# The ring of the near branch's value tiles: eight buffers in place of six

## The chip, the cores and the metric

The kernel runs on one core of one Trainium2 chip. The metric is device time in microseconds (us): the median of three runs before the change is 2152.53 (2151.78 to 2155.79).

## The reference: what is computed

A trunk of two residual layers over 1024 tokens of width 1024, all in fp32. Layer 0 mixes tokens with a chunked gMLP (mixer A) and with dilated sliding-window attention (mixer B), layer 1 with gated linear attention; behind each mixer stands a gated MLP with a short causal convolution. The change lies in mixer B of layer 0, cut here to what matters:

```python
B_HEADS = 8
B_HEAD_DIM = 64
B_BRANCHES = ((128, 1), (512, 4), (2048, 16))
B_BLOCK = 128
...
    qh = rms_norm(heads(q), q_g)
    kh = rms_norm(heads(k), k_g)
    vh = heads(vb).astype(jnp.float32)
    outs, lses = [], []
    for window, dilation in B_BRANCHES:
        o_r, l_r = dilated_branch(qh, kh, vh, window, dilation)
        outs.append(o_r)
        lses.append(l_r)
    wts = jax.nn.softmax(jnp.stack(lses), axis=0)
    o = jnp.einsum('rbhs,rbhsc->bhsc', wts, jnp.stack(outs))
    b_out = o.transpose(0, 2, 1, 3).reshape(Bn, S, B_WIDTH)
    return jnp.concatenate([a_out, b_out], axis=-1).astype(h.dtype) @ w_out
```

Each query sees a band of keys (its own block of 128 and the one before, at a stride), once for each branch; the branches' outputs are weighted by their denominators. The kernel computes the branch of dilation 1 as the "near" branch, and the two others as one "dilated" branch with a mask that counts them both.

## The kernel before, in words

**Layer 0's mixers** are the function `even` and what it calls. The eight heads go by pairs p = 0 to 3, the 1024 tokens by eight tiles n of 128.

`project(p)` makes q, k and v of a pair: for each token tile, `projected(n)` runs 24 matmuls of 128x384 into a PSUM tile `pj` (L193 at work for `mm_tok`), squares q and k into `qn` on ACT (L780), writes v times the token's norm into the value tile `vN` on ACT (L781 and L782), sends `vN` to a DRAM copy `vd` (L785), and scales q and k on DVE out of `pj` (L787 to L791). The value tiles are a ring: one pool tag `vN` with six buffers for all pairs. `qn` is a ring of five, `pj` one of two.

In the same loop the near branch's unit for tile n follows: splits and transposes of q and k (tiles `tq`, `tk`, L809 and L817), two score matmuls `sc` for each of two heads (L727), the mask and minimum on DVE (L732), the exponential on ACT (L733), transposes `pP` (L747), a copy `pT` (L750 or L752), and the value matmuls `po` (L755), which read `vN` of tiles n-1 and n. So a value tile n is free when the unit of tile n+1 has run.

`dilated(p)` runs eight such units on strided keys, with values `v4` read back from `vd`, into the tiles `ot..d`, and writes them to a DRAM tensor `od` (L849). They are read back in token order as `on` (L887). `combine` and `combined` weigh near and dilated outputs (L858 to L877: small operations on DVE, an exponential on ACT, three large multiplications and additions on DVE and POOL) and write the DRAM tensor `bcat` (L878).

**What fills TensorE beside the attention**: the projections of the next pair (`pj`), and for the last pair the gMLP's two projections `pv` and `pu` (eight tiles of 24 matmuls of 128x512 each, L193), with the small spatial matmuls `pm` (L678). Behind `pu` the output projection begins: `turn` transposes (tile `pc0`, L706) the first token tile's gMLP half (`mx`) and attention half (`cat`, read back from `bcat`, L697), the split into two fp32r parts goes to `hq` (L101 on ACT, L102 on DVE), and the matmuls `po0` follow (L193). `load_half` makes that projection's weights `wo0` by the same split (L101, L102) from DMA loads (L111).

**What sets the order.** The kernel is written with a tile framework that schedules: it lists the instructions of each engine in an order that follows a simulated timeline and the program's order as priority, and puts in the waits. Each engine then runs its own list strictly in order. A tile of a ring can be listed only behind the last reader of the buffer that it takes, so the number of buffers enters the order of every engine. Queue SP issues the DMAs, in order as well.

In the names below a number behind p stands for the pair, the next for the token tile: `pj10` is pair 1, tile 0; `po3d1` is the second output tile of pair 3's dilated branch.

Of the kernel before, what the change touches and what calls it, by code (L numbers as in the profile page):

```python
# [9 lines left out]
F32 = mybir.dt.float32  # L10
# [9 lines left out]
P = 128  # L20
# [23 lines left out]
def f32(ap):  # L44
    return ap.bitcast(F32)
# [6 lines left out]
def rows(t, n):  # L52
    return t[n * P : (n + 1) * P, :]
# [3 lines left out]
def trunk(ctx: ExitStack, tc: tile.TileContext, a, out):  # L57
# [41 lines left out]
    def split(dst, src, hi=None, lo=None):  # L99

        (hi or A.copy)(dst[0], src)  # L101
        (lo or V.tensor_sub)(dst[1], src, f32(dst[0]))  # L102
# [35 lines left out]
    def inv_rms(ssq, cols, n, name, r=None):  # L138
        if r is None:
            r = small.tile([P, cols], F32, tag="rs%d" % cols, name=name)  # L140
        G.tensor_scalar(r, ssq, 1.0 / n, EPS, op0=ALU.mult, op1=ALU.add)  # L141
        G.tensor_tensor(r, r, mhalf[:, :cols], op=ALU.pow)
        return r
# [36 lines left out]
    def tok(n, k):  # L180
        return [hq[k % 2][n // 4][:, i, k // 2, (n % 4) * P : (n % 4 + 1) * P] for i in range(2)]

    def mm_tok(ps, lhs, rhs, nk, amid=None):

        for k in range(nk):
            if amid and k == AMID:
                amid()
            L, R = lhs(k), rhs(k)
            for i in range(2):
                for o, sl in ps:  # L190
                    for ii, jj in PASSES:
                        if ii == i:
                            T.matmul(o, L[i], R[jj][:, sl], start=(k == 0 and (ii, jj) == PASSES[0]),  # L193
                                     stop=(k == nk - 1 and (ii, jj) == PASSES[-1]))
# [423 lines left out]
    def load_qkv(p, wx, between=None):  # L618

        ws = []  # L620
        for kp in range(4):
            raw = load_raw(a["w_qkv"][p, kp], f"wq{p}{kp}r", 768)
            if between:
                between(kp)
            for i in range(2):
                k = 2 * kp + i
                src, gain = raw[:, i * 384 : i * 384 + 384], g0[:, k : k + 1]
                if p % 2 or k >= 4:
                    ws.append(parts_of(src, f"wq{p}{kp}_{i}", gain=gain))
                else:  # L630
                    w = wx.tile([P, 2, 384], F32R, tag="wx", name=f"wx{p}{k}")
                    ws.append([w[:, j, :] for j in range(2)])
                    scaled(ws[-1], src, gain)
        return ws
# [80 lines left out]
    def attention(ps, at, av, pq, pq0, par0, wx, wq0, gqk, masks, rest, gm_open):  # L715
# [3 lines left out]
        def by4(t):  # L719

            return t.rearrange("p s (m r) -> p s r m", r=4)
# [36 lines left out]
        def outputs(name):  # L758
            return (at.tile([P, 4, 132], F32, tag="ot", name="ot" + name, bufs=6),
                    ps.tile([P, 4, P], F32, tag="po", name="po" + name))  # L760

        def project(p, ws=None, then=None, early=None):


            ws = ws or load_qkv(p, wx)
            pool = pq if p % 2 else pq0
            qR = pool.tile([P, 2, S], F32R, tag="qR", bufs=1, name=f"qR{p}")
            kT = pool.tile([P, 4, S], F32R, tag="kT", bufs=1, name=f"kT{p}")
            vd = dram.tile([S, P], F32, name=f"vd{p}")
            vN, os, qns = [], [], []  # L770
            heads = lambda t: t.rearrange("p (h c) -> p h c", c=64)

            def projected(n):

                pj = ps.tile([P, 512], F32, tag="pt" if early and n in (1, 3) else "pj", name=f"pj{p}{n}")
                mm_tok([(pj[:, :384], slice(0, 384))], lambda k: tok(n, k),
                       lambda k: ws[k], KD)
                qn = pq.tile([P, 256], F32, tag="qn", bufs=5, name=f"qn{p}{n}")
                rn = r0[:, n : n + 1]
                A.activation(qn, pj[:, :256], AF.Square, scale=rn)  # L780
                vN.append(pq.tile([P, P], F32, tag="vN", bufs=6, name=f"vN{p}{n}"))  # L781
                got = A.mul(vN[n], pj[:, 256:384], rn)  # L782
                if early:
                    early(n, got)
                Q.dma_start(rows(vd, n), vN[n])  # L785
                ssq = small.tile([P, 4], F32, tag="ss4", name=f"ss{p}{n}")
                V.reduce_sum(ssq, heads(qn), axis=AX.X)  # L787
                r = inv_rms(ssq, 4, 64, f"rq{p}{n}")
                V.scalar_tensor_tensor(heads(qn), heads(pj[:, :256]), rn, r[:, :, None].to_broadcast([P, 4, 64]),
                                       op0=ALU.mult, op1=ALU.mult)  # L790
                G.tensor_tensor(heads(qn[:, :P]), heads(qn[:, :P]), gqk[:, None, :].to_broadcast([P, 2, 64]), op=ALU.mult)  # L791
                qns.append(qn)

            lead = 3 if early else 0
            for n in range(lead):
                projected(n)
            for n in range(NT):
                if n + lead < NT:
                    projected(n + lead)
                qn = qns[n]  # L800
                qs = pq.tile([P, 2, P], F32R, tag="qs", bufs=2, name=f"qs{p}{n}")
                ks = pq.tile([P, 4, P], F32R, tag="ks", bufs=2, name=f"ks{p}{n}")
                split([qs[:, :, :64], qs[:, :, 64:]], heads(qn[:, :P]), hi=G.tensor_copy)
                kk = ks.rearrange("p (h i) (x c) -> p h i x c", i=2, x=2)
                split([kk[:, :, i] for i in range(2)], heads(qn[:, P:])[:, :, None, :].to_broadcast([P, 2, 2, 64]),
                      hi=G.tensor_copy)
                tq = ps.tile([P, 2, P], F32R, tag="tq", name=f"tq{p}{n}")
                for j in range(2):
                    T.transpose(tq[:, j, :], qs[:, j, :], identr)  # L809
                ts_ = slice(n * P, n * P + P)  # L810
                qT = pq.tile([P, 2, P], F32R, tag="qT", bufs=3, name=f"qT{p}{n}")
                A.copy(qT, f32(tq))
                four = lambda t: t.rearrange("p s (r m) -> p s r m", r=4)[:, :, :, 32 * n : 32 * n + 32]
                G.tensor_copy(four(qR), by4(f32(qT)))
                tk = ps.tile([P, 4, P], F32R, tag="tq", name=f"tk{p}{n}")
                for j in range(4):
                    T.transpose(tk[:, j, :], ks[:, j, :], identr)  # L817
                (V.tensor_copy if n % 2 else A.copy)(four(kT), by4(f32(tk)))

                if n % 4 == 0:  # L820
                    ot, po = outputs(f"{p}n{n}")
                    os.append(ot)
                m0 = max(n - 1, 0)
                unit(p, f"{p}n{n}", n % 4, ot, po, lambda s, qT=qT: qT[:, s],
                     lambda s, i: kT[:, 2 * s + i, :].rearrange("p (r m) -> p r m", r=4)[:, :, 32 * m0 : 32 * n + 32],
                     vN[m0 : n + 1], mband, lambda t: t.rearrange("p (m r) -> p r m", r=4))
                if n % 4 == 3:
                    A.copy(ot[:, :, :P], po)
                if then and n in (4, 5):
                    then(n - 4)  # L830
            v4 = av.tile([P, 4, 2, P], F32, tag="v4", name=f"v4{p}", bufs=1)
            for b in range(2):
                Q.dma_start(v4[:, :, b, :], vd.rearrange("(b m r) c -> b m r c", b=2, r=4)[b])
            return os, qR, kT, v4
# [46 lines left out]
        for p in range(PAIRS):  # L881
# [11 lines left out]
            def then(g):  # L893
                weights(g)()
# [470 lines left out]
```

## Time and profile before

| | |
|---|---|
| median of three runs | 2152.53 us |
| the profiled execution | 2153.15 us, its span 2151.4 us |
| PE busy | 2126.6 us (99%), 10444 matmuls |
| DVE, ACT, POOL busy | 1526.0 (71%), 1035.9 (48%), 482.4 us (22%) |
| mixers of layer 0 | from 0 to about 370 us of the span |

The profile is one execution. "Span" runs from the first to the last instruction; what lies around it (1.75 us here) belongs to the run's time. Busy shares are of the span. A matmul's row has a modelled end, so back-to-back matmuls overlap in the list. In the answers by stretches, (x158) is the number of instructions, PEclk the granted share of TensorE's clock, and PEld the loading of weights, which runs beside PE. In the timeline and the chain, a row is start, duration, engine, line and tiles; "SPq" is the issue of a DMA.

### The profile page before, as it was taken

Reading aid. Unit: us, or ns where it says so; the run is one execution under the profiler, and the core shown is the slowest. Engines: PE = TensorE matmul, PEld = TensorE weight load, DVE = VectorE, ACT = ScalarE, POOL = GpSimd, SP = SyncE. Lnnn points to the kernel's source line nnn. Section 1 sums busy time; section 2 is a strip of 40 time slices with the busy share of each in tenths; the row PEclk is TensorE's granted clock in tenths of the full one; section 3 lists DMA queues with packets and bytes.
Section 4 is the critical chain, followed back from the end, with each engine's and each line's share of the span. In section 5 each row is a group of like instructions: output and inputs, shape, how many; then the busy total and the mean of one; then the engine's idle time right before and its main releaser. Section 6 shows DMA issues by size and latency. Waiting matters only on the chain.

```text
span 2151.4 us, 29696 instructions
## 1 busy us (share of the span) xinstructions
PE 2126.6 (99%) x10444; PEld 1804.0 (84%) x10444; DVE 1526.0 (71%) x2451; ACT 1035.9 (48%) x1998; POOL 482.4 (22%) x521
## 2 busy tenths in 40 slices
PE   8999999999999999999999999999999999999999
PEld 7999988888888888888898888888788888888887
DVE  7566655587888888655577777677778888885554
ACT  7555664365444444444454455535544444444443
POOL 5344310012424334000010011011234334220000
PEclk9999999999999999999999999999999999999999
DMA  7022313754444544765553233395554544457664
GB/s 273 24 77 68 104 40 120 256 195 156 155 161 158 176 143 157 255 237 192 206 183 113 74 105 102 133 307 206 177 167 161 168 153 154 162 181 280 215 216 166
DMA packets 159413, 353.70 MB, mean 164 GB/s; under 512 B 17392, under 2 KB 54256, under 8 KB 158880
## 3 DMA queue, kind: packets, MB, share of 16 engines
q1 hardware_dynamic: 159264, 351.81, 47.9%
q8 instruction: 82, 1.34, 0.3%
q14 instruction: 67, 0.55, 0.1%
HBM read 243.15 MB, written 108.59 MB: 163 GB/s over the span
## 4 chain that ended last, share of the span: by engine, by line
PE 92%; DVE 2%; ACT 2%; DMA 2%; issue 1%; SPq 0%; POOL 0%; DVEq 0%; ACTq 0%
PE puB L293 11%; PE pgB L293 11%; PE po L193 8%; PE pv L193 6%; PE pj L193 6%; PE puC L293 6%; PE pgC L293 6%; PE pdB L400 5%; PE pdC L400 5%; PE pdO L400 4%; PE puA L293 3%; PE pgA L293 3%; PE pdQ L400 2%; PE pdP L400 2%; PE pu L193 2%; PE pBq L1070 2%
## 5 line engine op out<-in xcount | busy, mean ns | idle before, releaser
L102 DVE TENSOR_TENSOR da<-ar,da 128x512 fp32r<-128x512 f32 x154 | 106.1, 689 | 154.2 <-ACT da L101 154.1
L101 ACT CAST da<-ar 128x512 fp32r<-128x512 f32 x154 | 95.9, 623 | 207.8 <-PE pdC L400 91.5
L193 PE MATMUL po<-wo,hq 128*128 128x512 f32 x768 | 184.0, 394 | 0.2 <-ACT hq L101 0.2
L193 PEld LDWEIGHTS po<-wo,hq 128*128 128x128 f32 x768 | 141.6, 188 | 29.6 <-DVE hq L102 1.1
L193 PE MATMUL pv<-wv,hq 128*128 128x512 f32 (+2 forms) x768 | 140.8, 340 | 1.6 <-DVE b L1102 1.6
L400 PE MATMUL pdB<-dw,da 128*128 128x512 f32 x528 | 135.5, 391 | 0.9 <-ACT u L308 0.7
L400 PE MATMUL pdC<-dw,da 128*128 128x512 f32 x528 | 135.1, 390 | 0.0
L193 PEld LDWEIGHTS pv<-wv,hq 128*128 128x128 f32 x768 | 118.7, 189 | 16.4 <-DVE b L1102 2.1
L400 PEld LDWEIGHTS pdB<-dw,da 128*128 128x128 f32 x528 | 98.7, 188 | 22.3 <-ACT u L308 1.1
L259 POOL TENSOR_TENSOR S1g<-rg 128x512 f32<-128x512 f32 x20 | 31.1, 1555 | 382.9 <-DMA wsd<-D 266.1
L400 PEld LDWEIGHTS pdC<-dw,da 128*128 128x128 f32 x528 | 99.0, 188 | 20.5
L102 DVE TENSOR_TENSOR dw<-wr,dw 128x512 fp32r<-128x512 f32 x154 | 105.6, 686 | 12.1 <-ACT dw L101 11.9
L193 PE MATMUL pj<-wq,hq 128*128 128x384 f32 x576 | 111.3, 341 | 0.0
L141 POOL TENSOR_SCALAR rn<-ssq 128x1 f32<-128x1 f32 x24 | 9.7, 403 | 446.1 <-ACT h L149 244.9
L101 ACT CAST dw<-wr 128x512 fp32r<-128x512 f32 x154 | 95.0, 617 | 15.7 <-DMA wr<-in_w_dn 9.3
L400 PE MATMUL pdO<-dw,da 128*128 128x512 f32 x396 | 102.2, 389 | 0.2 <-DVE dw L102 0.2
L193 PEld LDWEIGHTS pj<-wq,hq 128*128 128x128 f32 x576 | 99.9, 189 | 0.1
L400 PEld LDWEIGHTS pdO<-dw,da 128*128 128x128 f32 x396 | 74.2, 188 | 16.0 <-DVE dw L102 0.6
L322 DVE SCALAR_TENSOR_TENSOR t<-g,cw,t 128x1022 f32<-128x1022 f32 x44 | 76.6, 1742 | 0.1
L306 DVE TENSOR_TENSOR g<-g,s1g 128x512 f32<-128x512 f32 x22 | 16.2, 737 | 76.9 <-ACT s1g L305 76.9
L321 DVE SCALAR_TENSOR_TENSOR t<-g,cw,t 128x1023 f32<-128x1023 f32 x44 | 58.2, 1322 | 16.2 <-ACT t L320 16.1
L323 ACT ACTIVATE t<-t 128x1024 f32<-128x1024 f32 x44 | 46.7, 1061 | 29.7 <-DVE t L322 29.6
(1084 smaller groups left out, 5432.6 us busy)
## 6 DMA issues: line engine op xcount, KB each, us to landing
ar<-actd SPq DMA_DIRECT2D x70, 512.0 KB, 3.5
rd<-in_w_down SPq DMA_DIRECT2D x44, 512.0 KB, 3.6
wsd<-D SPq DMA_DIRECT2D x88, 256.0 KB, 2.3
rg<-in_w_gate SPq DMA_DIRECT2D x42, 512.0 KB, 3.6
ru<-in_w_up SPq DMA_DIRECT2D x42, 512.0 KB, 4.5
wr<-wsd SPq DMA_DIRECT2D x40, 512.0 KB, 4.3
actd<-t SPq DMA_DIRECT2D x66, 256.0 KB, 2.2
wr<-in_w_dn SPq DMA_DIRECT2D x30, 512.0 KB, 4.8
```

The source lines that it names most:

```text
L101: (hi or A.copy)(dst[0], src)
L102: (lo or V.tensor_sub)(dst[1], src, f32(dst[0]))
L141: G.tensor_scalar(r, ssq, 1.0 / n, EPS, op0=ALU.mult, op1=ALU.add)
L193: T.matmul(o, L[i], R[jj][:, sl], start=(k == 0 and (ii, jj) == PASSES[0]), stop=(k == nk - 1 and (ii, jj) == PASSES[-1]))
L259: G.tensor_tensor(sums[name], x, y, op=op)
L293: T.matmul(o, L[ii][:, j * P : j * P + P], right[p][:, jj, j, :], skip_group_check=more, start=(not more and j == 0 and (ii, jj) == PASSES ...
L306: V.tensor_add(C22, C22, s1)
L321: V.scalar_tensor_tensor(t[:, 1:], g[:, : S - 1], w(1), t[:, 1:], op0=ALU.mult, op1=ALU.add)
L322: V.scalar_tensor_tensor(t[:, 2:], g[:, : S - 2], w(0), t[:, 2:], op0=ALU.mult, op1=ALU.add)
L323: A.activation(t, t, AF.Silu)
L400: T.matmul(o, L[ii][:, t * P : t * P + P], R[jj], skip_group_check=more, start=start and not more and (ii, jj) == PASSES[0], stop=stop and ...
L1070: T.matmul(o, L[ii][:, j * P : j * P + P], right[p][:, jj, j, :], skip_group_check=more, start=(not more and j == 0 and (ii, jj) == PASSES ...
```

## The change

One number: the ring `vN` gets eight buffers of 128x128 fp32 (512 bytes in each partition) in place of six.

```diff
@@ -778,7 +778,7 @@
                 qn = pq.tile([P, 256], F32, tag="qn", bufs=5, name=f"qn{p}{n}")
                 rn = r0[:, n : n + 1]
                 A.activation(qn, pj[:, :256], AF.Square, scale=rn)
-                vN.append(pq.tile([P, P], F32, tag="vN", bufs=6, name=f"vN{p}{n}"))
+                vN.append(pq.tile([P, P], F32, tag="vN", bufs=8, name=f"vN{p}{n}"))
                 got = A.mul(vN[n], pj[:, 256:384], rn)
                 if early:
                     early(n, got)
```

No instruction of the computation is added or removed; ACT gets two more loads of its function tables (31 in place of 29). But the lists of all engines change, from pair 0's near units to the output projection. Three places matter.

**First, PE at pair 0's near units 1 and 2.** Before, this stood there (`pP`, `sc`, `po` are the units' transposes, scores and values; `pj10` is the next pair's first projection):

```order
L747 MATMUL pP0n1_704<-ident_73,sm0n11_716 128x128 x2
L817 MATMUL tk03_854<-identr_78,ks03_843 128x128 x4
L755 MATMUL po0n0_625<-vN00_469,pT0n1_721 128x64
L755 MATMUL po0n0_625<-vN01_510,pT0n1_721 128x64
L755 MATMUL po0n0_625<-vN00_469,pT0n1_721 128x64
L755 MATMUL po0n0_625<-vN01_510,pT0n1_721 128x64
L747 MATMUL pP0n2_782<-ident_73,sm0n20_786 128x128 x2
L727 MATMUL sc0n30_861<-kT0_440,qT03_851 128x256 x2
L727 MATMUL sc0n31_869<-kT0_440,qT03_851 128x256 x2
L809 MATMUL tq04_927<-identr_78,qs04_921 128x128 x2
L747 MATMUL pP0n2_782<-ident_73,sm0n21_794 128x128 x2
L193 MATMUL pj10_1309<-wq10_0_1276,hq00_85 128x384 x3
```

With eight buffers, this stands behind the last projection `pj07` of pair 0:

```order
L809 MATMUL tq02_770<-identr_78,qs02_764 128x128 x2
L193 MATMUL pj07_884<-wq03_1_370,hq11_88 128x384
L193 MATMUL pj10_1309<-wq10_0_1276,hq00_85 128x384 x3
L193 MATMUL pj10_1309<-wq10_1_1279,hq10_87 128x384 x3
L193 MATMUL pj10_1309<-wq11_0_1284,hq00_85 128x384 x3
L193 MATMUL pj10_1309<-wq11_1_1287,hq10_87 128x384 x3
L193 MATMUL pj10_1309<-wq12_0_1292,hq00_85 128x384 x3
L193 MATMUL pj10_1309<-wq12_1_1295,hq10_87 128x384
L817 MATMUL tk02_776<-identr_78,ks02_765 128x128 x4
```

The projection `pj10` moved up from behind unit 1's value matmuls (the last readers of `vN00`) and unit 2's transposes to directly behind `pj07`. From there on, projections stand about two token tiles earlier against the near units in every pair.

The moves add up to longer and shorter stretches without a large matmul (`pj`, `pv` or `pu`). Before, between `pj17` and `pj20` stood 116 small matmuls, between `pj27` and `pj30` 108, between `pj37` and `pv0` 106, and 32 between `pj07` and `pj10`. Now the longest are 101 (between `pj21` and `pj22`) and 86 (between `pj31` and `pj32`); between `pj37` and `pv2` none has more than 24.

**Second, PE at the end of the attention.** `po3d1<-...pT3d13` is the last value matmul of pair 3's last dilated unit. Before:

```order
L193 MATMUL pu3_4429<-wu1_1_4294,hq10_87 128x512 x3
L193 MATMUL pu3_4429<-wu2_0_4299,hq00_85 128x512
L755 MATMUL po3d1_3824<-v43_3725,pT3d13_3903 128x64 x4
L678 MATMUL pm02_4108<-mx0_3957,ws_3954 128x256 x2
L678 MATMUL pm04_4112<-mx0_3957,ws_3954 128x256 x2
L193 MATMUL pu3_4429<-wu2_0_4299,hq00_85 128x512 x2
```

and, 101 `pu` matmuls and 14 `pm` matmuls behind it, the transposes of the output projection:

```order
L193 MATMUL pu7_4545<-wu2_1_4302,hq11_88 128x512 x3
L706 MATMUL pc00_4564<-ident_73,mx0_3957 128x128 x2
L706 MATMUL pc00_4564<-ident_73,cat00_4513 128x128 x2
L706 MATMUL pc01_4571<-ident_73,mx0_3957 128x128 x2
L706 MATMUL pc01_4571<-ident_73,cat00_4513 128x128 x2
L193 MATMUL pu7_4545<-wu3_0_4307,hq01_86 128x512 x3
L193 MATMUL pu7_4545<-wu3_1_4310,hq11_88 128x512 x3
L193 MATMUL po00_4658<-wo00_0_4610,hq00_85 128x512 x3
```

With the change, the last value matmul stands here:

```order
L747 MATMUL pP3d13_3886<-ident_73,sm3d131_3898 128x128 x2
L678 MATMUL pm02_4108<-mx0_3957,ws_3954 128x256 x2
L755 MATMUL po3d1_3824<-v43_3725,pT3d13_3903 128x64 x4
L678 MATMUL pm04_4112<-mx0_3957,ws_3954 128x256 x2
L678 MATMUL pm06_4116<-mx0_3957,ws_3954 128x256 x2
L678 MATMUL pm10_4265<-mx1_3958,ws_3954 128x256 x2
L678 MATMUL pm12_4269<-mx1_3958,ws_3954 128x256 x2
L193 MATMUL pu7_4545<-wu0_0_4283,hq01_86 128x512 x3
```

and the transposes here, with 24 `pu`, 12 `pm` and the four pairs of transposes of `mx` between:

```order
L193 MATMUL pu7_4545<-wu3_1_4310,hq11_88 128x512 x3
L678 MATMUL pm14_4273<-mx1_3958,ws_3954 128x256 x2
L678 MATMUL pm16_4277<-mx1_3958,ws_3954 128x256 x2
L706 MATMUL pc00_4564<-ident_73,mx0_3957 128x128 x2
L706 MATMUL pc01_4571<-ident_73,mx0_3957 128x128 x2
L445 MATMUL pc10_4644<-ident_73,mx0_3957 128x128 x2
L445 MATMUL pc11_4651<-ident_73,mx0_3957 128x128 x2
L706 MATMUL pc00_4564<-ident_73,cat00_4513 128x128 x2
L706 MATMUL pc01_4571<-ident_73,cat00_4513 128x128 x2
L445 MATMUL pc10_4644<-ident_73,cat01_4640 128x128 x2
L445 MATMUL pc11_4651<-ident_73,cat01_4640 128x128 x2
L193 MATMUL po00_4658<-wo00_0_4610,hq00_85 128x512 x3
```

Of the work that stood between the last attention unit and the first transpose of `cat00`, `pu3` to `pu6` moved ahead of the last unit; the rest of `pu7`, which stood between the transposes and `po00`, moved ahead of the transposes.

**Third, DVE at the weighing of pair 3's branches** (`cM`, `cE`, `cD` are small tiles of weights, `on` and `ot` the two branches' outputs, `wo` the output projection's weights). Before:

```order
L858 TENSOR_TENSOR cM30_4369<-ot3n0_3122,on30_3912 128x8
L692 TENSOR_TENSOR mx0_3957<-mx0_3957,ut2_4426 128x512
L692 TENSOR_TENSOR mx0_3957<-mx0_3957,ut3_4454 128x512
L861 TENSOR_TENSOR cE30_4371<-cM30_4369,ot3n0_3122 128x8
L861 TENSOR_TENSOR cE30_4371<-cM30_4369,on30_3912 128x8
L858 TENSOR_TENSOR cM31_4375<-ot3n4_3433,on31_3914 128x8
L861 TENSOR_TENSOR cE31_4377<-cM31_4375,ot3n4_3433 128x8
L861 TENSOR_TENSOR cE31_4377<-cM31_4375,on31_3914 128x8
L869 TENSOR_TENSOR cD30_4381<-cE30_4371,ot3n0_3122 128x8
L869 TENSOR_TENSOR cD30_4381<-cE30_4371,on30_3912 128x8
L870 TENSOR_TENSOR cD30_4381<-cD30_4381 128x8
L871 RECIPROCAL cD30_4381<-cD30_4381 128x8
```

Now:

```order
L858 TENSOR_TENSOR cM30_4369<-ot3n0_3122,on30_3912 128x8
L102 TENSOR_TENSOR wo00_0_4610<-wo00r_4608,wo00_0_4610 128x512
L102 TENSOR_TENSOR wo00_1_4613<-wo00r_4608,wo00_1_4613 128x512
L861 TENSOR_TENSOR cE30_4371<-cM30_4369,ot3n0_3122 128x8
L861 TENSOR_TENSOR cE30_4371<-cM30_4369,on30_3912 128x8
L858 TENSOR_TENSOR cM31_4375<-ot3n4_3433,on31_3914 128x8
L102 TENSOR_TENSOR wo01_0_4618<-wo01r_4616,wo01_0_4618 128x512
L102 TENSOR_TENSOR wo01_1_4621<-wo01r_4616,wo01_1_4621 128x512
L861 TENSOR_TENSOR cE31_4377<-cM31_4375,ot3n4_3433 128x8
L861 TENSOR_TENSOR cE31_4377<-cM31_4375,on31_3914 128x8
L102 TENSOR_TENSOR wo02_0_4626<-wo02r_4624,wo02_0_4626 128x512
L869 TENSOR_TENSOR cD30_4381<-cE30_4371,ot3n0_3122 128x8
```

The eight `wo` splits, which stood behind the whole weighing, moved into it; the other four of them, two `mx` additions (L680) and two `mx` multiplications (L692) follow between the rows of `cD` before the large multiplications `on30` and `on31` (L875) and the additions (L877), which end it. Behind the first of these additions SP writes `bcat0` and then reads `cat00`, as before.

## The prediction

> **What bounds the kernel now.** I read the busy shares first, then the chain that ended last.
>
> ```profile
> PE 2126.6 (99%) x10444; PEld 1804.0 (84%) x10444; DVE 1526.0 (71%) x2451; ACT 1035.9 (48%) x1998; POOL 482.4 (22%) x521
> ...
> PE 92%; DVE 2%; ACT 2%; DMA 2%; issue 1%; SPq 0%; POOL 0%; DVEq 0%; ACTq 0%
> ```
>
> TensorE is busy for 99% of the span and carries 92% of the chain. A reordering can therefore gain only where PE stands or runs slowly, and it loses wherever PE comes to wait. No matmul is added, so the sum has two terms: S, what is lost now in stretches of small matmuls, and W, a new wait. The stretches that the change shortens, and three for comparison, answer by windows:
>
> ```profile
> 9.80:15.20 5.40, 5.34 (x17) 5.34 (x18) 4.21 (x8) 4.44 (x9) 1.44 (x3) 1.00 0.95 369
> 15.20:20.60 5.40, 5.40 (x33) 5.40 (x32) 3.35 (x9) 3.02 (x7) 1.57 (x4) 1.00 1.03 416
> 47.00:56.00 9.00, 7.54 (x50) 6.69 (x49) 7.50 (x22) 5.77 (x18) 4.85 (x9) 0.82 0.55 183
> 52.60:56.10 3.50, 3.50 (x19) 3.50 (x20) 2.32 (x6) 1.50 (x7) 1.02 (x3) 0.52 0.21 72
> 105.00:124.00 19.00, 18.88 (x158) 17.64 (x157) 15.08 (x53) 17.15 (x56) 5.01 (x9) 1.00 0.48 146
> 170.00:188.00 18.00, 17.59 (x146) 16.58 (x146) 13.61 (x47) 15.75 (x52) 5.09 (x10) 1.00 0.37 111
> 235.00:252.00 17.00, 15.91 (x129) 14.54 (x127) 12.95 (x43) 15.26 (x47) 5.69 (x9) 1.00 0.74 224
> ```
>
> Only the first of the four attention stretches, 47 to 56 us, shows gaps and a granted clock under 1. What causes it is in the timeline:
>
> ```profile
> 52.49 1.77 PE L755 MATMUL po0n<-vN,pT0n 128*128 128x64 f32 x8
> ...
> 53.87 0.37 ACT L782 ACTIVATE vN<-pj,r 128x128 f32<-128x128 f32 x1 [0.45 <-PE po0n L755]
> 55.85 1.44 PE L193 MATMUL pj<-wq,hq 128*128 128x384 f32 x6
> ```
>
> Unit 1's value matmuls free a buffer of the ring; ACT then fills it from `pj`, and only later does the next projection start. That is the ring of six at work.
>
> **Part one: the projections earlier, the gain S.** The window at 105 is dense: 158 matmuls in 19.00 us, 8.3 per us. At that rate the 50 matmuls of the first stretch take 6.0 us, so 3.0 of its 9.0 are lost, 3.50 x (1 - 0.52) = 1.7 of these to the clock. The 129 of the last stretch take 15.5, so 1.5 of 17.0 are lost; the 146 at 170 take 17.6, 0.4 lost. The order puts `pj10` straight behind `pj07`, and leaves no more than 24 small matmuls in a row where the last stretch was: I take both losses as saved, S = 3.0 + 1.5 = **4.5 us**. The two middle stretches only shrink (116 to 101 matmuls, 108 to 86) and I give them nothing. Bounds: 0, if the gaps only move; and if all idle time of the weight loads in the four stretches went, 2.3 + 1.4 + 1.4 + 2.5 (length less PEld's busy time), with the 1.7 of clock 9.2 us.
>
> **Part two: the attention later, the wait W.** The chain at the end of the attention:
>
> ```profile
> 337.42 0.84 PE po3d L755 x8
> 338.26 1.78 PE pm L678 x8
> ...
> 350.45 0.87 PE pm L678 x4
> ...
> 357.87 9.56 PE pu L193 x42
> 367.44 0.87 PE pc L706 x8
> 368.31 1.39 PE pu L193 x6
> 369.70 2.32 PE po L193 x10
> ```
>
> The last unit ends at T = 338.26, and `cat` is wanted at about 367.4: 29.2 us of `pu` and `pm` cover the way from the unit's output through DRAM, the weighing, DRAM again and back. With the change 24 `pu` (24 x 9.56/42 = 5.5), 12 `pm` (8 at 1.78, 4 at 0.87) and 8 transposes of `mx` (0.9) are left: **9.0 us**. The work that left the cover runs before T, so it is not lost; only what the cover fails to hide is. The way itself:
>
> ```profile
> 338.30 0.59 ACT L847 COPY ot3d<-po3d 128x512 f32<-128x512 f32 x1 [3.11 <-PE po3d L755]
> 339.22 0.89 SPq L849 DMA_DIRECT2D od<-ot3d  x2
> 342.82 0.91 SPq L887 DMA_DIRECT2D on<-od  x2
> 347.84 0.15 DVE L858 TENSOR_TENSOR cM<-ot3n,on 128x8 f32<-128x8 f32 x1
> 349.43 1.28 ACT L862 ACT_TABLE_LOAD   x1 [6.13 <-DVE cM L858]
> 350.98 0.17 DVE L869 TENSOR_TENSOR cD<-cE,ot3n 128x8 f32<-128x8 f32 x1 [1.27 <-ACT cE L862]
> 354.87 0.69 DVE L875 TENSOR_TENSOR on<-on,cE 128x512 f32<-128x512 f32 x1
> 354.91 1.55 POOL L875 TENSOR_TENSOR ot3n<-ot3n,cE 128x512 f32<-128x512 f32 x1 [32.54 <-DVE cE L872]
> 356.50 0.69 DVE L877 TENSOR_TENSOR ot3n<-ot3n,on 128x512 f32<-128x512 f32 x1
> 360.48 1.29 DVE L692 TENSOR_TENSOR mx<-mx,ut 128x512 f32<-128x512 f32 x2
> 364.78 1.32 DVE L102 TENSOR_TENSOR wo<-wo00r,wo 128x512 fp32r<-128x512 f32 x2
> 368.00 1.07 ACT L101 CAST hq<-pc 128x512 fp32r<-128x512 f32 x2
> 368.74 1.28 DVE L102 TENSOR_TENSOR hq<-pc,hq 128x512 fp32r<-128x512 f32 x2
> ```
>
> and the landings of its transfers in this part of the trace (size of one, median us from issue to landing):
>
> ```profile
> on<-od SPq DMA_DIRECT2D x2, 264.0 KB, 3.0
> bcat<-ot3n SPq DMA_DIRECT2D x2, 256.0 KB, 2.5
> cat<-bcat SPq DMA_DIRECT2D x3, 256.0 KB, 3.0
> ```
>
> With the change, counted from T:
> - `od` is issued at +0.96 and `on` at +4.56 (both as now, 339.22 and 342.82), and lands 3.0 later: +7.6.
> - DVE then runs its list up to the end of the first L877. Between stand eight `wo` splits (8 x 0.66 = 5.3), two L680 and two L692 (about 4 x 0.66 = 2.6), sixteen small operations (0.15 to 0.17 each alone, less where they overlap; 0.14, 2.2) and the end: from the first large multiplication to the first addition's end the trace has 354.87 to 357.19, 2.3; 2.4. Together 12.5: +20.1. ACT's exponential and its table load of 1.28 lie beside the `wo` splits.
> - `bcat` lands 2.5 later, +22.6, `cat` 3.0 after that: **+25.6**.
>
> PE, done at +9.0, waits 16.6 us. Then the split of `pc00` into `hq` has no cover: now six `pu` of 1.39 lie beside it; the transposes of `pc10` and `pc11` cover about 0.4, 1.0 stays. W = 17.6. After such a gap PE should start slowly. The trace has two slow stretches: 1.7 us in the row at 52.60, and the kernel's start, 17 matmuls in 5.40 us where the next 5.40 have 33, 2.6 lost. I take the middle, 2.2.
>
> Such a drop has a rule. The Trainium skill, in "TensorE: Matmul & The Clock Gate", section "Part 1: The HAM clock gate", says that TensorE falls to half its clock after about one idle window of 3.4 us and is released after some 3.4 us of sustained work; the estimate by that page is 1.7 us for each drop and the sum would be 0.5 us lower. The granted 0.52 over 3.50 us agrees with it.
>
> **The other edits.** ACT's two further table loads stand beside PE's projections, where ACT has slack (48% busy): nothing, and 2 x 1.28 = 2.6 us if that cover were missing. Two more buffers change no transfer. Behind the attention PE has no slack to win the delay back: it stays the chain to the end, so the whole of it arrives there.
>
> **Sum:** 17.6 + 2.2 - 4.5 = **+15.3 us** on the profiled execution's 2153.15 (its span 2151.4), 2168.45. The median shown is 0.6 lower, 2152.53; against it, 2167.8, I write **2168**.
>
> **The rivals.**
>
> *A shorter chain.* The `wo` splits and `mx` operations stand early in DVE's list, but their inputs may come so early, or the `on` landing so late, that they don't add: the chain loses 5.3 + 2.6 = 7.9, and the time is about 2160. Against it: the order puts all of them behind `cM30`, which waits for `on`, and DVE runs strictly in order.
>
> *A longer one.* Nothing of S appears (the middle stretches still hold 101 and 86 small matmuls), and the loads of `wo10` to `wo13`, now issued ahead of `bcat`, slow its write and the read of `cat` by a microsecond or two: 2168 + 4.5 + 2 = about 2174. For it: the row at 235 already shows 0.74 of the DMA engines busy.
>
> *Faster.* All four stretches give their bound, 9.2 us, and the tail costs only its bare hops: 0.96 + 3.6 + 3.0 + 2.5 + 3.0 = 13.1 against 9.0 of cover, so 4.1 of wait and no drop of the clock: -5, 2147 to 2148. It decides as soon as the way behind the last unit is shorter than cover plus S, 9.0 + 9.2 = 18.2 us at best and 13.5 with my S; the trace of now needs 339.22 - 338.26 + 3.6 + 3.0 and then, at DVE's present pace, more than 9 for the weighing, so I hold it unlikely. The Trainium skill, in "Perfetto Trace Analysis", section "Optimization Strategy", speaks for this rival: consistent bubbles on the engine that should be saturated can mean too few buffers for the next tile. The timeline at 53.87 shows just such a wait, but only in one place of a few microseconds.
>
> *No change.* The order moves, but `pj10` and its followers wait for something else (a PSUM buffer, `qn`, ACT), and the chain at the tail is short: the 15.3 less 7.9 and less the other 4.7 of S's bound, +2.7, is still within what can't be told from nothing.
>
> **How the numbers follow.** A measurement of this kernel can tell about 0.2%, 4.3 us, from no change. The forecast, 2164 to 2173, gets 0.74; the shorter chain 0.10; the longer 0.08; faster 0.04; no change 0.04. The range takes in the shorter chain (2160) and the longer (2174), each with 3 us for the bounds of its terms (S and the clock's restart), and drops the two last: 2157 to 2177. Faster 0.04, same 0.04, slower 0.92.
>
> **What would show it.** In the new profile the granted clock stays at 1 around 47 to 56 us and `pj10` follows `pj07` without a gap. Behind the last `po3d`, PE runs some 9 us and then stands 16 to 18 us, released by the DMA `cat<-bcat`, with a low granted clock right behind. The first `po` starts about 15 us after its 369.70. DVE shows `wo` splits between `cM` and the large multiplications of L875. From there to the end all rows are shifted alike. The prediction is wrong if PE has no gap ahead of `pc`, if the gap lies elsewhere, or if S is far from 4.5: then the stretches, or the waits of `pj`, tell why.

## The result, and the profile after

With eight buffers the kernel takes 2164.8 us (median of six runs, 2163.3 to 2170.37) against 2153.72 before (six runs, 2151.78 to 2156.41): the medians are 11.1 us apart, and the ratio taken over all executions is 1.0058, 95% interval 1.0048 to 1.0068, which is 12.5 us, 10.3 to 14.6. 2168 with 2157 to 2177 was forecast. The profiled execution is the slowest of the six, 2170.37 us with a span of 2168.7; its first 391 us are read here. Two executions far out of line, 3046 us in e7 and 4759 us of the kernel before beside e5 to e8, enter the medians below but not the ratios.

The first page, busy shares and the head of the chain:

```profile
PE 2129.1 (98%) x10444; PEld 1805.6 (83%) x10444; DVE 1527.5 (70%) x2451; ACT 1038.3 (48%) x2000; POOL 483.9 (22%) x521
...
PE 88%; DMA 4%; DVE 4%; ACT 3%; issue 1%; SPq 0%; POOL 0%; DVEq 0%; ACTq 0%
```

TensorE does the same 10444 matmuls and its share of the chain falls from 92% to 88%: DMA and DVE have each gone from 2% to 4%. Where the early stretches were, and at the tail (from the last attention unit to the output projection's matmuls `po`), the windows of the changed kernel (stretch, length, PE, PEld, DVE, ACT, POOL, granted clock, DMA share, GB/s) are:

```profile
47.00:56.00 9.00, 9.00 (x63) 8.93 (x62) 7.26 (x20) 6.53 (x18) 5.24 (x10) 1.00 0.67 203
113.40:128.60 15.20, 15.19 (x131) 14.02 (x129) 11.86 (x43) 12.76 (x44) 5.39 (x12) 1.00 0.29 78
236.00:253.00 17.00, 16.93 (x107) 14.84 (x107) 5.16 (x24) 8.14 (x26) 2.25 (x5) 1.00 0.25 81
369.00:375.00 6.00, 0.18 (x1) 0.00 (x0) 5.56 (x9) 0.05 (x1) 3.04 (x2) 0.50 0.40 141
375.00:378.00 3.00, 0.01 (x1) 0.02 (x1) 0.00 (x0) 0.00 (x0) 0.00 (x0) 0.50 0.71 221
381.40:388.20 6.80, 6.80 (x27) 5.53 (x26) 1.29 (x2) 1.07 (x2) 0.00 (x0) 0.78 0.35 127
388.00:394.00 6.00, 6.00 (x32) 5.09 (x31) 1.98 (x3) 1.07 (x2) 0.00 (x0) 1.00 0.27 90
```

At 47 to 56 us PE is full and the clock is whole. At 369 to 378 it does next to nothing (0.19 us), with the clock at 0.50. Only behind 388 does it run as before. The timeline of PE at that place, with what released it:

```profile
351.68 1.00 PE L755 MATMUL po3d<-v,pT3d 128*128 128x64 f32 x8
352.52 3.86 PE L678 MATMUL pm<-mx,ws 128*128 128x256 f32 x16
356.69 5.74 PE L193 MATMUL pu<-wu,hq 128*128 128x512 f32 x24 [0.31 <-ACT ut L691]
362.27 1.89 PE L678 MATMUL pm<-mx,ws 128*128 128x256 f32 x8
367.04 1.29 PE L706 MATMUL pc<-ident,mx 128*128 128x128 f32 x4 [2.88 <-DVE mx L680]
368.12 1.06 PE L445 MATMUL pc<-ident,mx 128*128 128x128 f32 x4
377.99 1.11 PE L706 MATMUL pc<-ident,cat 128*128 128x128 f32 x4 [8.80 <-DMA cat<-bcat]
380.75 1.11 PE L445 MATMUL pc<-ident,cat 128*128 128x128 f32 x4 [1.65 <-DMA cat<-bcat]
381.52 7.06 PE L193 MATMUL po<-wo,hq 128*128 128x512 f32 x24
```

The last unit ends at 352.7. Behind it come 24 `pu`, 24 `pm` and 8 transposes of `mx`, and then two waits for a DMA. The 2.88 us in which PE waits for `mx` ahead of them cost nothing of their own here, because `cat` is still 11 us away. The chain from there shows the way that the two waits hang on:

```profile
351.85 0.85 PE po3d L755 x8
...
353.64 3.75 DMA od<-ot3d
...
357.40 3.17 DMA on<-od
...
360.69 0.99 DVE wo L102 x2
...
366.39 1.20 DVE mx L680 x2
...
371.23 1.54 DVE ot3n L877
...
372.79 2.35 DMA bcat<-ot3n
...
376.06 4.65 DMA cat<-bcat
...
381.87 1.28 PE po L193 x3
```

Two transfers through DRAM, 12 us of DVE, two transfers again. The last DMA row is `cat01`, the second token tile's half, not the first one's; `cat00` is there at 377.99.

**A ledger of lost time.** To compare kernels with different orders I give each matmul up to `po` the time that its form usually takes to the next one's start (the median over the traces: 0.227 us for 128x512, 0.174 for 128x384, 0.216 for `pm`, 0.11 to 0.12 for most small ones). What the trace needs beyond that is lost; a drop of the clock counts as lost too. Cut at equal amounts of work done, in us:

| kernel | near units of pair 0 | the two middle stretches and between | last stretch ahead of `pv` | units of pair 3 | tail up to `po` |
|---|---|---|---|---|---|
| before | 4.0 | 4.5 | 3.0 | 0.7 | -0.4 |
| changed | 0.1 | 4.3 | 0.5 | 1.5 | 17.5 |
| e1, only pair 3 | 2.5 | 4.4 | 0.1 | 3.1 | 17.5 |
| e2, only pairs 0 to 2 | 0.1 | 4.3 | 3.1 | 0.5 | -0.3 |
| e3, lockstep | 0.1 | 4.1 | 0.5 | 13.7 | 0.1 |
| e4, wo behind | 0.1 | 4.5 | 0.6 | 1.6 | 11.8 |
| e5, seven | 0.8 | 3.6 | 0.4 | 1.7 | 14.3 |
| e6, catch up | 0.1 | 4.0 | 0.6 | 8.7 | 2.9 |
| e8, five | 3.3 | 5.0 | 0.7 | 0.4 | 7.7 |

Changed less before: 3.9 and 0.2 and 2.5 won in the stretches, 0.8 and 17.9 lost from pair 3's units on: 12.1 us, and at 391 us of the changed kernel's span the same matmul of both kernels stands 12.45 us apart. The ledger is of one execution each, and e1 shows how far that goes at pair 0.

### The profile page after: what moved, and what is told of

It is laid out like the page before. It is cut to its first block, busy times and chain, and to the rows that moved or that the text cites. A ratio compares the mean times of both kernels' runs of the same rounds, so it can differ in the third digit from the quotient of the medians.

```text
span 2168.7 us, 29701 instructions
## 1 busy us (share of the span) xinstructions
PE 2129.1 (98%) x10444; PEld 1805.6 (83%) x10444; DVE 1527.5 (70%) x2451; ACT 1038.3 (48%) x2000; POOL 483.9 (22%) x521
## 4 chain that ended last, share of the span: by engine, by line
PE 88%; DMA 4%; DVE 4%; ACT 3%; issue 1%; SPq 0%; POOL 0%; DVEq 0%; ACTq 0%
PE pgB L293 11%; PE puB L293 11%; PE pv L193 6%; PE pj L193 6%; PE pgC L293 5%; PE puC L293 5%; PE pdB L400 5%; PE pdC L400 5%; PE pdO L400 4%; PE po L193 4%; PE pgA L293 3%; PE puA L293 3%; PE pdQ L400 2%; PE pdP L400 2%; PE pu L193 2%; PE pBq L1070 2%
## 5 line engine op out<-in xcount | busy, mean ns | idle before, releaser
L102 DVE TENSOR_TENSOR dw<-wr,dw 128x512 fp32r<-128x512 f32 x154 | 105.8, 687 | 10.3 <-ACT dw L101 9.7
```

## The experiments

Theory: two separate effects. The earlier projections fill stretches of small matmuls (gain), and the last attention unit stands too close to the transposes that need its result (loss). Rivals: the loss comes from the attention of all pairs standing later; the gaps only move; the transfers alone set the wait.

**e1 and e2: each half of the change alone.** Two of the eight buffers get a tag of their own, which only some pairs use; the other pairs have a ring of six. This is e1; e2 has `two = p < 3 and n > 5`.

```diff
-                vN.append(pq.tile([P, P], F32, tag="vN", bufs=8, name=f"vN{p}{n}"))
+                two = p == 3 and n > 5
+                vN.append(pq.tile([P, P], F32, tag="vX" if two else "vN", bufs=2 if two else 6, name=f"vN{p}{n}"))
```

> Six buffers for pairs 0 to 2, eight for pair 3 alone (two more under a tag of their own). Its list of TensorE is that of the six-buffer kernel up to pair 3 and that of the changed kernel at the tail: 11.5 us of fill between the last attention unit and the transposes of cat. Theory (the loss is the exposed way of the last unit through DRAM, the gain lies in the stretches that the earlier projections fill): the whole tail, about 18 us, less the last stretch (2.6): 15 to 17 us over the kernel before, so slower than the changed kernel by about 4. Rival (the loss comes from all pairs, their attention standing later against the projections): only a quarter to a half of the change's 12, 3 to 6 us over before.

Measured: 2170.74 us against 2152.65, 1.0085 (1.0072 to 1.0097), 18 us over: above the theory's 15 to 17, which its interval of 15.5 to 20.9 reaches, and far from the rival's 3 to 6. The ledger has 15.8 of them, and at 391 us of its span the profiled execution is 16.25 us behind the one of before. Its PE row at the tail:

```profile
381.45 1.12 PE L706 MATMUL pc<-ident,cat 128*128 128x128 f32 x4 [8.64 <-DMA cat<-bcat]
```

This run also says what pair 0's 4.0 are. Up to 235 us TensorE's order is that of the kernel before, and the first stretch has its gaps, but not its drop of the clock:

```profile
47.00:56.00 9.00, 7.55 (x58) 6.70 (x57) 8.35 (x25) 6.99 (x22) 5.43 (x11) 1.00 0.58 184
```

58 matmuls at a granted clock of 1.00 stand here, where the profiled execution of before has 50 at 0.82, and 2.5 us are lost in place of 4.0. So 1.5 us of pair 0's loss in the ledger is a drop of the clock that the same order of TensorE need not show; about 2.4 is what the waits for a buffer cost.

> Eight buffers for pairs 0 to 2, six for pair 3. The tail has 26.4 us of fill again and no split of wo stands in the weighing. Theory: only the gain at pair 0's near units is left (3.9 us), the stretch ahead of pv0 is a little longer (128 matmuls for 106, about 0.5 lost), the way from the last unit to cat (about 21 us) is covered: 3 to 4 us under the kernel before. Rival (the loss comes from all pairs): 5 to 9 us over before. Rival (the gaps only move, no gain): within 1 us of before.

Measured: 2149.57 us against 2152.65, 0.9984 (0.9976 to 0.9993): 3 us faster, as the theory had it. It is the only version here that beats both kernels. Part of the 3 us is probably the clock: of the 15 executions of before beside it, the seven with a mean granted clock of 1.000 took 2149.83 to 2152.22 us and the eight with 0.998 or 0.999 took 2152.65 to 2155.84, while all eleven of e2 show 1.000. Where in the span the clock fell in them is not on record. Its timeline at the tail has no wait:

```profile
356.78 7.19 PE L193 MATMUL pu<-wu,hq 128*128 128x512 f32 x30
363.82 0.38 PE L706 MATMUL pc<-ident,mx 128*128 128x128 f32 x2
364.03 0.38 PE L706 MATMUL pc<-ident,cat 128*128 128x128 f32 x2
...
366.08 4.29 PE L193 MATMUL po<-wo,hq 128*128 128x512 f32 x18
```

So the loss belongs to pair 3, and a gain remains without it, at pair 0 by the ledger. The gaps do not only move.

**e3 and e6: eight buffers, and the fill held behind the units of pair 3.** `issue_after` puts the matmuls of a `pv` or `pu` tile behind a named value matmul on TensorE.

```diff
+            with tc.issue_after(done[behind[f"{name}{n}"]].ins) if f"{name}{n}" in behind else nullcontext():
+                mm_tok([(pj, slice(0, 512))], lambda k: tok(n, k), lambda k: ws[k], KD, amid if n == NT - 1 else None)
...
+        behind.update({'pv3': '3n0', 'pv4': '3n1', 'pv5': '3n4', 'pv6': '3n6', 'pv7': '3n6', 'pu0': '3d01', 'pu1': '3d01', 'pu2': '3d11', 'pu3': '3d13', 'pu4': '3d13', 'pu5': '3d13', 'pu6': '3d13', 'pu7': '3d13'})
...
+                    done[name] = T.matmul(po[:, i, 64 * s : 64 * s + 64], pT[:, s, j, :], vb[j][:, 64 * s : 64 * s + 64],
```

> Eight buffers for all pairs, and the fill of pair 3 held in step with its units: pv3 to pv7 and pu0 to pu7 issue behind value matmuls of named near and dilated units, pu3 to pu7 behind the last one. Cover at the tail 32.1 us, no stretch of more than 26 small matmuls in pair 3. Theory: the gain stays whole and the tail costs nothing: 5 to 7 us under the kernel before, about 18 under the changed kernel. Rival (what the earlier projections gain is given back when the units have to be waited for): within 2 us of before.

Measured: 2162.68 us (2157.9 to 2163.59) against 2152.65, 1.0044 (1.0031 to 1.0056): 10 us slower. My expectation missed by 16 us, and the rival's 2 us were too few as well. The tail lost nothing, as meant, but 13.7 us went at pair 3's units. The windows and two rows of its timeline (the profiled execution was the fastest of the five):

```profile
268.00:297.00 29.00, 23.91 (x133) 20.38 (x133) 22.52 (x62) 11.84 (x29) 8.85 (x15) 0.88 0.06 19
```

```profile
277.11 0.74 PE L731 MATMUL sc3n<-kT,qT 128*128 128x256 f32 x4 [2.74 <-DVE kT L822]
...
292.27 0.44 PE L751 MATMUL pP3n<-ident,sm3n 128*128 128x128 f32 x2 [1.22 <-ACT sm3n L737]
```

PE waits for what DVE and ACT make of the unit before; DVE is busy for 22.5 of 29 us there, and 29.00 x (1 - 0.88) = 3.5 us of clock go with it.

> Eight buffers; the fill of pair 3 is held behind its units as in the lockstep kernel, but only from pv5 on and looser, so that the attention catches up by some three fill tiles over its thirteen units instead of at once; 23.3 us of fill stand behind the last unit, and three large operations of DVE in the weighing. Theory: cat lands some 20 us after the last unit and is covered; the gain of 6.4 us stays but for 1 to 3 us of waits for units: 3 to 5 us under the kernel before. Rival (any pull of the attention makes TensorE wait for a unit's own chain, as the lockstep run showed): at or over the kernel before, up to 10 us.

Its map is `{'pv5': '3n2', 'pv6': '3n4', 'pv7': '3n5', 'pu0': '3n6', 'pu1': '3d00', 'pu2': '3d02', 'pu3': '3d10', 'pu4': '3d12', 'pu5': '3d13', 'pu6': '3d13', 'pu7': '3d13'}`. Measured: 2158.81 us against 2153.71, 1.0025 (1.0015 to 1.0036): 5 us slower, the rival's case. 8.7 us are lost at pair 3's units and 2.9 at the tail. The window and the longest waits of its timeline:

```profile
290.00:313.00 23.00, 18.91 (x107) 15.88 (x107) 18.60 (x46) 19.30 (x35) 3.60 (x9) 0.98 0.32 104
```

```profile
309.97 0.44 PE L731 MATMUL sc3d<-kT,qR 128*128 128x128 f32 x2 [1.46 <-DVE ot3d L736]
311.97 0.69 PE L751 MATMUL pP3d<-ident,sm3d 128*128 128x128 f32 x2 [1.56 <-ACT sm3d L737]
```

Packed closer, the units come near the pace of DVE (18.6 of 23 us busy) and ACT (19.3); spread over the fill as before, they cost PE 0.7 us in all. The fill between the units hides them, so in these two orders what was saved for the tail was paid for ahead of it. Other orders were not tried.

**e4: the weighing without the `wo` splits.**

```diff
-            V.tensor_add(o0, o0, o1)
+            weighed[g] = V.tensor_add(o0, o0, o1)
...
-        wo = load_half(w[0], "wo0")
+        with nullcontext() if l else tc.issue_after(weighed[1].ins):
+            wo = load_half(w[0], "wo0")
```

> Eight buffers, and the eight subtractions that make wo0 are issued on DVE behind the last addition of the weighing. Theory: DVE's list is part of the tail's way: without the splits (5.3 us) and what moves with them cat lands 5 to 7 us earlier, and as the cover is 10.8 us, all of it shows: 5 to 7 us under the changed kernel, 5 to 8 over before. Rival (the transfers through DRAM alone set the wait): within 1 us of the changed kernel, 12 over before.

Measured: 2161.78 us against 2152.65, 1.0042 (1.0028 to 1.0055): 9 us over before, 2 to 3 under the changed kernel, less than expected; the two intervals overlap, so the trace has to decide. Its PE timeline:

```profile
351.21 1.00 PE L758 MATMUL po3d<-v,pT3d 128*128 128x64 f32 x8
...
370.81 0.69 PE L709 MATMUL pc<-ident,cat 128*128 128x128 f32 x2 [3.24 <-DMA cat<-bcat]
372.89 0.69 PE L709 MATMUL pc<-ident,mx 128*128 128x128 f32 x2 [1.40 <-DVE mx L683]
```

`cat` is there 18.6 us after the last unit (352.2) in place of 25.3: 6.7 us, within the theory's 5 to 7. But an addition on `mx` had come to stand behind the `wo` splits on DVE, PE waits for it, and the ledger wins 5.7 of the 6.7. The rival, the transfers alone, is out: they would have left the wait as it was. Profiled, the kernel stands 5.9 us behind before at 391 us of its span and 9.7 at its end; of the other 4, up to 1.7 can be a row of 3.5 us at a granted clock of 0.51 from 1533.8; where the rest went isn't settled.

**e5 and e8: seven and five buffers** (only the number in the `vN` line changes).

> Seven buffers. The stretches of pair 0's near units and ahead of pv0 are gone as with eight; the tail has 17.3 us of fill where the changed kernel has 11.5 and the six-buffer kernel 29.2, and 15 large operations of DVE stand in the weighing (12 in the changed kernel). Theory (time = gain of the stretches, less what the tail's way exceeds the fill): cat lands about 27 us after the last unit, 10 us of wait, with the split into hq and the clock 14 to 15, less 6.4: 7 to 10 us over the kernel before. Rival (the gain needs all eight, the loss comes with any move): as the changed kernel, 12 over.

Measured: 2163.89 us against 2153.71, 1.0047 (1.0035 to 1.006): 10 us over, at the edge of the theory's 7 to 10. Its interval, 7.5 to 12.9 us, overlaps the change's own of 10.3 to 14.6, so only the ledger separates it from the rival: tail 14.3 in place of 17.5. `cat` comes 29 us after the last unit, later than the 27 expected.

> Five buffers. The stretches without a large matmul have 46, 100, 100 and 80 small ones (32, 116, 108 and 106 with six), the tail has 20.8 us of fill, and three large operations of DVE stand in the weighing. Theory: cat lands about 20 to 21 us after the last unit, so only the split into hq and a little more is exposed: 0 to 4 us over the kernel before. Rival (the number of buffers itself costs: a smaller ring only makes waits): 5 us or more over it, from the stretches.

Measured: 2160.82 us against 2153.71, 1.0034 (1.0021 to 1.0046): 7 us over, outside the theory's 0 to 4. By the ledger the rival is wrong too: the stretches cost 2.5 less than before, the tail 8.1 more. The way exceeded the fill by 2 us only, but a second wait follows in PE's timeline:

```profile
368.54 0.44 PE L706 MATMUL pc<-ident,cat 128*128 128x128 f32 x2 [2.00 <-DMA cat<-bcat]
...
373.37 0.69 PE L445 MATMUL pc<-ident,cat 128*128 128x128 f32 x2 [3.74 <-DMA cat<-bcat]
```

The order puts the transposes of `cat01` ahead of `po00`, and `cat01` comes 4.8 us behind `cat00`. With six buffers these transposes stand behind the first matmuls of `po00`, where nothing waits for them.

**e7, e9 and e10: the clock behind the wait.** Forty matmuls whose result is not used fill part of the wait; `turned` is the last transpose of `mx` ahead of it.

```diff
+            warm = ps.tile([P, 512], F32, tag="sc", name="warm")
+            with tc.issue_after(turned.ins):
+                for i in range(40):
+                    T.matmul(warm, wu[0][0][:, :P], wu[0][0], start=(i == 0), stop=(i == 39))
+            V.tensor_copy(scrap, warm[:, :8])
...
+        scrap = small.tile([P, 8], F32, tag="scrap", bufs=1, name="scrap")
```

> The changed kernel with 40 matmuls of 128x512 on loaded weights, 9.1 us, whose result is not used (one copy of 8 columns reads it), between the last transpose of mx and the first of cat, where TensorE waits anyway. Theory: TensorE comes out of the wait at full clock, so the transposes of cat and the first matmuls of po00 run at their usual rate: 1 to 2.5 us under the changed kernel. Rival (the low clock costs nothing, because the first work behind the wait is bound by the split into hq): within 0.5 us of it.

Measured: 2180.58 us against 2153.71, 1.0125 (1.0106 to 1.0143): 27 us over, where neither theory was. At 390 us of its span the kernel is 2.6 us ahead of the changed one; the rest goes later. The new tile `scrap` adds 32 bytes to a pool ahead of most others, so I took it out (e9: `tag="bn"`, an existing ring, 6 columns) and put it in alone (e10: `pad` 16 columns wide in place of 8, nothing else).

> As the run with the 40 filling matmuls, but their result is read into a tile of a ring that exists already (6 columns), so that no tile of SBUF moves. That run came out of the wait 2.6 us earlier than the changed kernel by its profile and then lost 16 us evenly in the gated MLPs' up projections (L293). Theory (the 32 bytes of the new small tile moved every tile behind it, and the matmuls of L293 read more slowly from there): the loss is gone, 1 to 3 us under the changed kernel, 9 to 11 over before. Rival (the filling matmuls cost something later): again 25 us or more over before.

Measured: 2164.56 us against 2153.66, 1.0051 (1.0037 to 1.0064): 11 us over. The loss is gone. Against the changed kernel's 1.0058 that is 1.5 us less, with overlapping intervals; the clock's price is read from the row of the 6.80 us in which `po00` begins, shown above for the changed kernel with 27 matmuls at 0.78:

```profile
381.40:388.20 6.80, 6.80 (x38) 5.79 (x37) 1.98 (x3) 1.45 (x3) 0.00 (x0) 1.00 0.51 189
```

and of the two `po` rows: 24 matmuls in 7.06 us there, and here

```profile
381.64 5.71 PE L193 MATMUL po<-wo,hq 128*128 128x512 f32 x24
```

1.35 us on `po00`. It did not come out as a difference of times that stands by itself. `po00` begins no earlier than in the changed kernel (381.52), although the clock is whole: it still has to wait for `cat01`.

> The changed kernel with nothing but the small tile named pad 16 columns wide in place of 8, 32 bytes more in each partition; every engine's list is the same. Theory (placement): 14 to 18 us over the changed kernel, lost in L293. Rival: no difference to the changed kernel.

Measured: 2180.83 us against 2153.66, 1.0127 (1.0113 to 1.014): 27 us over, 15 to 16 more than the changed kernel, with every engine's list the same. The windows 560 to 680 us (up projections of the MLP), the changed kernel's and this one's:

```profile
560.00:680.00 120.00, 120.00 (x531) 99.37 (x530) 103.45 (x110) 54.93 (x89) 47.02 (x26) 1.00 0.47 156
```

```profile
560.00:680.00 120.00, 120.00 (x521) 97.52 (x520) 101.58 (x107) 53.76 (x87) 45.01 (x25) 1.00 0.46 153
```

Ten matmuls fewer in 120 us at a full clock, 1.9%. The ring's own two buffers, 1024 bytes more, could have had such a price as well. They have none here, as the same window of the kernel before shows:

```profile
560.00:680.00 120.00, 120.00 (x532) 99.34 (x531) 99.09 (x106) 53.79 (x88) 43.72 (x24) 1.00 0.47 157
```

## Why the prediction was right

It gave 15.3 us by a gain of 4.5 and a loss of 19.8; the ledger has a gain of 6.6 and a loss of 18.7, and 12.5 us were measured (11.1 by the medians). Mechanism, place and sign held; several terms had the wrong size, and that the sum comes as near as it does is in part luck, since the errors go both ways.

- **Gain S, 4.5: too small.** Pair 0's near units gave 3.9 where 3.0 was forecast, and the last stretch 2.5 where 1.5 was. But the forecast took the 1.7 of clock in its 3.0 for an effect of the ring of six, and e1 has TensorE's order of that ring there without the drop: some 2.4 of the 3.9 are waits. The rate of 8.3 per us came from the window at 105, which itself contains lost time (1.5 us by the ledger between the cuts around it), so it was no clean measure. That the two middle stretches gain nothing held (0.2).
- **Cover, 9.0: too small.** Real: 24 `pu`, 24 `pm`, 8 transposes, 24 x 0.227 + 24 x 0.216 + 0.9 = 11.5. The 12 `pm` were counted in the order's list, where one `pm` matmul shows as two in the trace. The chain of before has 28 `pm` between T and the transposes where the list has 14: the two views had only to be laid side by side. And where one gap of 16 to 18 us was forecast, three stand: 2.88 for `mx`, 8.80 for `cat00` and 1.65 for `cat01`.
- **The way, +25.6: +25.3.** `od` at +0.94, `on` at +4.70, the first weighing at +7.9, the end of the first addition at +20.1 (forecast +20.1), `cat` at +25.3. Its parts held less well than their sum: from the first large multiplication to the end of the first addition it took 3.6 us (369.18 to 372.77) where 2.4 was forecast, as the second multiplication of `on` stands between and both it and the addition took 1.53; DVE's other operations ahead of it took 8.6 where 10.1 was. e4 shows that the `wo` splits and what moved with them belong to the way: without them +18.6.
- **Split into `hq`, 1.0: 3.5.** From the arrival of `cat` at 377.99 to `po` at 381.5. The prediction saw the transposes of `pc10` as cover; they stand in line ahead of `po00` and wait 1.65 us for a transfer of their own. e8 shows the same, 3.74 us. Of the 3.5, 0.9 is the transposes' own work, which is not lost.
- **Restart of the clock, 2.2: about 1.35 at `po00`** and a little on the transposes ahead of it, which take 1.11 us for four in the changed kernel (0.60 in e9). The low clock is there, at 0.50. The Trainium skill, in "TensorE: Matmul & The Clock Gate", section "Part 1: The HAM clock gate", has half the clock after an idle window of about 3.4 us and the whole one after as long a busy one; the row at 381.40 agrees, 6.80 x (1 - 0.78) = 1.5 us. The two rows of the forecast do not bear the rule out as the forecast says. The one at 52.60 agrees in length alone: PE was no idle engine ahead of that drop (49.33 to 52.74, busy for 2.26 of 3.41 us), and at the same place in e1 (49.5 to 53), where no drop came, it was busy for 2.36 of 3.50 us. And the row at 9.80, from which the 2.6 was taken, shows a granted clock of 1.00.
- **The rest.** The added table loads show in no row of the chain above. No later stage gives the delay back. The first `po` starts 12 us later than before, not 15. The profiled execution has another 4.8 us behind the tail, which, by their times, four of the other five runs don't have; up to 1.7 of them can be a row of 3.5 us at a granted clock of 0.51 from 1531.2.
- **The rivals.** A shorter chain failed as argued: the splits stand behind `cM30` and add. The faster rival's first half is real in part: fewer waits for a buffer, up to the 6.6 of the ledger. What the Trainium skill says in "Perfetto Trace Analysis", section "Optimization Strategy", of bubbles that mean too few buffers holds at pair 0's near units: by the ledger e2 wins 3.9 us there, some 2.4 of them waits. Its second half, a tail of bare hops, would have needed 13.1 in place of 25.3 us; even e4 has 18.6.

The net by parts: S 2.1 more than forecast, the wait for `cat` 13.8 in place of 16.6, the split 2.5 more, the clock 0.9 less: 15.3 - 2.1 - 2.8 + 2.5 - 0.9 = 12.0. That this meets the ledger's 12.1 is in part luck: 0.9 of the transposes' own work is counted in it and the 0.8 lost at pair 3's units is not, and the two nearly cancel.

## What to carry to other kernels

In a kernel whose order follows from when buffers come free, more buffers move work forward, and the work that moved is missing where it used to hide something: look for the last producer whose result goes the long way, and count the work left behind it. Give the extra buffers only to the stages that wait for them (e2), and remember that fill kept back for the end is fill taken from the units before it (e3, e6). Before a drop of the clock is put down to a change, see whether another execution of the same order has it (e1). When a tile is added for an experiment, hold the addresses of all others still, or run the shift alone.

## What the runs showed that I had not expected

32 bytes more in a small pool, with identical lists of instructions, cost 15 to 16 us of 2165 (e10 against the change; e7 against e9), spread over the MLPs' up projections (L293): about 1.9% fewer matmuls in the same time at a granted clock of 1.00. Which operand's address does it was not tried.
